# Down projection of a hybrid block: 30 instead of 26 groups by seven products, with two and four weight sums in turn

## The chip, the core and the metric

The kernel runs on one core of a Trainium2 chip. The metric is the device time of one execution in microseconds (us), lower is better. Three runs of the kernel before took 1469.24 to 1470.96 us, with a median of 1470.67 us.

## The reference, cut to what matters

A transformer block with three kinds of attention and a gated feed-forward part works on 256 rows of width 2048, in float32. The change concerns the feed-forward part alone:

```python
h2 = rms_norm(x, g_ffn[l])
u = causal_depthwise_conv(h2 @ w_up[l], conv_w[l], conv_b[l])   # w_up: 2048 x 11264
u_gate, u_val = jnp.split(u, 2, axis=-1)
x = x + (jax.nn.silu(u_gate) * u_val) @ w_down[l]               # w_down: 5632 x 2048
```

## The kernel before, in words

**Numbers in two parts.** TensorE multiplies in a reduced form of float32. So every weight tile is split on the chip: ScalarE casts it (`hi`), VectorE subtracts (`lo`), and one product of two 128-row blocks is three matmuls of 128x512: hi by hi, lo by hi, hi by lo (`three`). A weight tile of 128x1024 is 512 KB.

**The up stage** (lines 1242 to 1267 of the kernel before) runs over 11 blocks of 4 columns of 128, each once for the gate half and once for the value half, and each of these over 8 pieces of `w_up`: 176 pieces in all. A piece is loaded by SyncE's queue into one of 4 buffers (`raw_u`, line 177), cast by ScalarE (`hi_u`, line 180), subtracted by VectorE (`lo_u`, line 181), and used by 8 matmuls of 512 columns (line 1254) and 8 of 256 (line 1256). There are 4 buffers of `hi` and 4 of `lo`, so the piece that is prepared can be up to four ahead of the one that is multiplied. The convolution (`conv`, lines 1135 to 1180) reads the finished banks with ScalarE and VectorE. The order of these instructions on each engine is made by a scheduler, except where the code keeps an instruction in program order.

**The down stage** multiplies 22 groups of two row blocks of `w_down`, in two halves (`nb`) of 1024 output columns. A group can be done in two ways:

- `eight`: 8 products, 24 matmuls, two tiles of 512 KB loaded, cast and subtracted.
- `seven`: a scheme after Strassen with 7 products, 21 matmuls. It needs four sums of the activations ("forms", `FS1` to `FS4`) and four sums of the weights (`T1` to `T4`). It casts and subtracts three and a half tiles.

**The forms** are made in the up stage by VectorE (`forms_of`, `keep_forms`), written to HBM by GpSimd's queue (`kept`), and fetched back in the down stage into ten slots in SBUF (`sf`, 384 KB each, `fetch`). A group that is done by seven products in both halves needs three stored forms; one that is so done in the second half alone needs the fourth as well.

**The weight sums** come in two kinds, by a letter in `PLANS`:

- `t` ("two"): `weight_sums` makes T4 and T2 in the up stage, with 3 additions of 128x512 on VectorE, and GpSimd's queue writes them to HBM as one tile (`T0`, 512 KB). T1 and T3 are added in the down stage by VectorE (line 1371). The group loads 3 tiles of 512 KB.
- `f` ("four"): all four are made in the up stage, with 4 additions, and written as two tiles (`T0` and `T1`). The group loads 256 KB and 3 tiles of 512 KB, and adds nothing in the down stage.

`weight_sums` is a generator that the up stage steps once a piece: one load of 256 KB of `w_down` in each of four steps (buffers `r0`, one copy, and `r1`, two copies), additions in the sixth and seventh, writes in the seventh and eighth. SyncE's queue carries the loads of `r0` and `r1` between those of `raw_u`, and a load into a buffer that is still being written to HBM holds up everything behind it on that queue.

**`PLANS`** gives the order of the groups: `e` is a group by eight, `t` and `f` are groups by seven. Each group becomes two (`e`) or four (`t`, `f`) steps; the loads and casts of a step are issued two steps ahead, and `at(n, ...)` issues a fetch behind step n. Loads from the eleventh on alternate between two pools of four buffers each; the first ten use one pool of four.

Of the kernel before, what the change touches and what calls it, by code (L numbers as in the profile page):

```python
# [34 lines left out]
SBUFS = 4  # L35
BLOCKS = 14
WINDOW = 2
PLANS = ("eeeee" + "tfte" * 3 + "tft" + "ee", "e" + "tte" * 4 + "tfte" + "tftee")
AHEAD = 2
GATE_PLANS = (("e" * 8, "essessee", "essessee"), ("eeesssee", "essessee", "essessee"))  # L40
GATE_SEVENS = 4
# [6 lines left out]
OUT_SEVENS = 3  # L48
KINDS = tuple(plan.replace("e", "") for plan in PLANS)
NSEVEN = tuple(len(kinds) for kinds in KINDS)  # L50
# [8 lines left out]
def hybrid_block(  # L59
# [62 lines left out]
    def later(gen):  # L122
        waiting.append(gen)
# [48 lines left out]
    def piece(src, a, n, name):  # L172
        raw = wp.tile([P, PIECE], F32, tag="raw", name=f"raw_{name}")
        hi = wp.tile([P, PIECE], F32R, tag="hi", bufs=SBUFS, name=f"hi_{name}")
        lo = wp.tile([P, PIECE], F32R, tag="lo", bufs=SBUFS, name=f"lo_{name}")
        m = a * n
        load = nc.sync.dma_start(raw[:, :m].rearrange("p (a n) -> p a n", a=a), src)
        if pinned[0] or in_order[0]:
            tc.keep_in_program_order(load)
        pin(nc.scalar.copy(hi[:, :m], raw[:, :m]))  # L180
        pin(nc.vector.tensor_tensor(lo[:, :m], raw[:, :m], hi[:, :m].bitcast(F32), ALU.subtract))  # L181
        return (
            hi[:, :m].rearrange("p (a n) -> p a n", a=a),
            lo[:, :m].rearrange("p (a n) -> p a n", a=a),
        )
# [924 lines left out]
    def two_banks(name):  # L1110
        return pp2[0].tile([P, 2, 512], F32, tag="pair", name=name)
# [87 lines left out]
    ended = []  # L1199
    made = {}  # L1200
    asked = [(nb, s) for nb in range(2) for s in range(NSEVEN[nb])]
    n_asked = len(asked)

    def weight_sums(nb, s):
        p = ORDERS[nb][s]
        n0 = nb * PIECE
        r = [
            cps[2].tile([P, 2, 512], F32, tag=f"r{j}", bufs=1 + j, name=f"r{j}_{nb}_{p}") for j in range(2)
        ]
        for j, n in ((1, 1), (1, 0), (0, 1), (0, 0)):  # L1210
            tc.keep_in_program_order(
                nc.sync.dma_start(r[j][:, n], dv[:, 2 * p + j, n0 + n * 512 : n0 + (n + 1) * 512])
            )
            yield 1
        yield 1
        add = lambda o, i: tc.keep_in_program_order(nc.vector.tensor_tensor(o, o, i, ALU.add))
        four = KINDS[nb][s] == "f"
        add(r[0][:, 0], r[0][:, 1])
        if four:
            add(r[0][:, 1], r[1][:, 1])  # L1220
        yield 1
        add(r[1][:, 1], r[0][:, 0])
        add(r[1][:, 0], r[1][:, 1])
        made[nb, p] = [dram.tile([P, PIECE], F32, name=f"T{j}_{nb}_{p}") for j in range(1 + four)]
        if four:
            nc.gpsimd.dma_start(made[nb, p][1], r[0].rearrange("p b n -> p (b n)"))
        yield 1
        nc.gpsimd.dma_start(made[nb, p][0], r[1].rearrange("p b n -> p (b n)"))

    adding, n_ticks = [], [0]  # L1230
# [11 lines left out]
    for f0 in range(0, FT, 4):  # L1242
        for s in range(2):
            pairs = [two_banks(f"u{f0 + i}_{s}") for i in (0, 2)]
            c0 = s * D_FF + f0 * P
            for k in range(0, KT, 2):
                hi, lo = piece(upv[:, k : k + 2, c0 : c0 + 512], 2, 512, f"u{f0}_{s}_{k}")
                for j in range(2):
                    first, last = k + j == 0, k + j == KT - 1
                    for i, part in ((0, hi), (1, hi), (0, lo), (1, lo), (2, hi), (3, hi), (2, lo), (3, lo)):  # L1250
                        ps = pairs[i // 2][:, i % 2]
                        c = slice(i * P, (i + 1) * P)
                        if part is hi:
                            nc.tensor.matmul(ps, lhsT=hi[:, j, c], rhs=hT[:, k + j, :], start=first, stop=False)  # L1254
                        else:
                            nc.tensor.matmul(ps[:, :S], lhsT=lo[:, j, c], rhs=hT[:, k + j, :S], start=False, stop=last)  # L1256
                n_ticks[0] += 1
                due = (n_ticks[0] - 8) * n_asked // 164
                if asked and due > n_asked - len(asked):
                    adding.append([weight_sums(*asked.pop(0)), 0])  # L1260
                add_on()
                tick()
            if not cps:
                conv_pool()
            for i in (0, 2):
                later(conv(pairs[i // 2], f0 + i, s))
# [43 lines left out]
    def fetch(p):  # L1310
        slot_of[p] = free_slots.pop(0)
        keep(nc.sync.dma_start(sf[:, slot_of[p]].bitcast(F32), kept[p][:, :, : 3 * P].bitcast(F32).rearrange("p l (f q) -> p l f q", f=3)))
        if p >= NSEVEN[0]:
            keep(nc.sync.dma_start(form_of(p, FS4).bitcast(F32), kept[p][:, :, 3 * P :].bitcast(F32)))
# [152 lines left out]
    def at(n, do):  # L1467
        after_step.setdefault(n, []).append(do)

    to_fetch = list(range(SLOTS, NSEVEN[0])) + list(ORDERS[1][SLOTS:])  # L1470
    for nb, plan in enumerate(PLANS):
        n0 = nb * PIECE
        ns, s = NSEVEN[nb], 0
        X, Y = (lambda nb=nb: banks[nb][0]), (lambda nb=nb: banks[nb][1])
        straight = list(range(FT // 2 - 1, ns - 1, -1)) if nb else list(range(ns, FT // 2))
        n_done = 0
        if nb == 0:
            at(-1, lambda: start(0))
            for p in range(SLOTS):
                at(1 + 2 * p if p < 4 else 3 * p - 4, lambda p=p: fetch(p))  # L1480
        for i, c in enumerate(plan):
            if c != "e":
                p = ORDERS[nb][s]
                seven(p, c, n0, X, Y, s == 0, s == ns - 1)
                if to_fetch and (nb or p < NSEVEN[0] - SLOTS):
                    at(len(steps) + 7, lambda p=p, q=to_fetch.pop(0): (free_slots.append(slot_of.pop(p)), fetch(q)))
                s += 1
                if s == ns:
                    at(len(steps) - 1, lambda nb=nb: later(gather(nb, banks[nb][1])))
            else:  # L1490
                eight(straight.pop(0), n0, X, i == 0, i == len(plan) - 1)
                n_done += 1
                if n_done == 4:
                    at(len(steps) - 1, lambda nb=nb: residual(nb))
        assert s == ns and not straight
        at(len(steps) - 1, finish)
        at(len(steps) - 1, lambda nb=nb: results(nb))
        if nb == 0:
            at(len(steps) - 1, lambda: start(1))
# [45 lines left out]
```

## Time and profile before

| what | value |
|---|---|
| median of three runs | 1470.67 us |
| the profiled execution | 1470.68 us |
| its span (first to last instruction) | 1468.7 us |
| up stage, first to last matmul | 749.6 to 1242.0 us |
| down stage, first to last matmul | 1242.1 to 1464.3 us |
| matmuls of the down stage | 978 |
| granted TensorE clock | 1.00 |

The profile names a group of instructions by line, engine, operation, and tiles as output<-input. `PE` is TensorE, `DVE` VectorE, `ACT` ScalarE, `POOL` GpSimd, `SPq` the queue of SyncE, which issues most of the loads. Matmuls overlap in the records: the time that one costs is read from the starts of successive ones, not from its length. The same holds for VectorE, where the starts of successive instructions lie closer than their lengths.

### The profile page before, as it was taken

How to read it: one execution, taken by the hardware profiler on the slowest of the kernel's cores; microseconds unless marked ns; L12 is line 12 of the kernel's file. 1: busy time of each engine (PE TensorE's matmuls, PEld its weight loads, DVE VectorE, ACT ScalarE, POOL GpSimd, SP SyncE). 2: the span in 40 equal slices, each digit the busy share in tenths (PEclk: the TensorE clock that was granted, in tenths of full speed). 3: DMA queues.
4: the chain of work that ended last, by engine and by line, in shares of the span. 5: the costliest groups of instructions: out<-in, count | busy, mean ns of one | idle time of the engine just before them, and what ended most of it. 6: DMA issues, size and time to landing. Idle time of an engine off the chain costs nothing.

```text
span 1468.7 us, 20884 instructions
## 1 busy us (share of the span) xinstructions
PE 1460.2 (99%) x7315; PEld 1230.6 (84%) x7315; DVE 1210.1 (82%) x1609; ACT 897.6 (61%) x1281; POOL 82.7 (6%) x165
## 2 busy tenths in 40 slices
PE   9999999999999999999999999999999999999998
PEld 7888887888878888888888888888888888888887
DVE  5798766765998799888877888988888888889988
ACT  6755454454664465555667676777676676665664
POOL 1000000021000000000000110100000001000000
PEclk9999999999999999999999999999999999999999
DMA  8698897797666577866766989999988888998985
GB/s 295 200 337 266 264 315 260 225 305 271 233 228 200 204 266 258 284 212 232 276 225 222 305 300 318 300 313 316 297 300 285 289 272 287 397 340 310 339 301 180
DMA packets 172329, 404.82 MB, mean 276 GB/s; under 512 B 14944, under 2 KB 27536, under 8 KB 172224
## 3 DMA queue, kind: packets, MB, share of 16 engines
q1 hardware_dynamic: 156080, 356.62, 72.0%
q0 software_dynamic: 15392, 45.82, 8.5%
q8 instruction: 57, 0.93, 0.3%
q10 hardware_dynamic: 752, 1.06, 0.2%
q14 instruction: 48, 0.39, 0.1%
HBM read 360.97 MB, written 42.47 MB: 275 GB/s over the span
## 4 chain that ended last, share of the span: by engine, by line
PE 96%; DVE 2%; DMA 1%; issue 0%; ACT 0%; SPq 0%; DVEq 0%; ACTq 0%
PE u L1254 22%; PE u L1256 11%; PE d L1325 5%; PE d L1326 5%; PE d L1327 5%; PE g_x L774 4%; PE g_x L775 4%; PE g_x L776 4%; PE f L193 2%; PE f L191 2%; PE f L192 2%; PE s L191 2%; PE s L192 2%; PE s L193 2%; PE b L193 2%; PE b L192 2%
## 5 line engine op out<-in xcount | busy, mean ns | idle before, releaser
L1254 PE MATMUL u<-hT,hi_u 128*128 128x512 f32 x1408 | 442.6, 396 | 0.0
L1256 PEld LDWEIGHTS u<-hT,lo_u 128*128 128x128 f32 x1408 | 264.5, 188 | 62.4
L1256 PE MATMUL u<-hT,lo_u 128*128 128x256 f32 x1408 | 276.9, 278 | 0.0
L181 DVE TENSOR_TENSOR lo_u<-raw_u,hi_u 128x1024 fp32r<-128x1024 f32 x176 | 213.1, 1220 | 47.1 <-ACT hi_u L180 46.3
L180 ACT CAST hi_u<-raw_u 128x1024 fp32r<-128x1024 f32 x176 | 183.4, 1049 | 106.4 <-DMA raw_u<-in_w_up_dram 47.7
L1254 PEld LDWEIGHTS u<-hT,hi_u 128*128 128x128 f32 x1408 | 214.5, 189 | 0.1
L769 ACT CAST hi_g<-raw_g 128x1024 fp32r<-128x1024 f32 (+1 forms) x96 | 91.2, 964 | 55.0 <-PE g_x L775 35.0
L770 DVE TENSOR_TENSOR lo_g<-raw_g,hi_g 128x1024 fp32r<-128x1024 f32 (+1 forms) x96 | 105.0, 1116 | 20.5 <-ACT hi_g L769 20.3
L774 PE MATMUL g_x<-hi_g,xT 128*128 128x512 f32 x251 | 98.8, 394 | 0.0
L775 PE MATMUL g_x<-hi_g,xT 128*128 128x512 f32 x251 | 97.7, 389 | 0.0
L776 PE MATMUL g_x<-lo_g,xT 128*128 128x512 f32 x251 | 96.3, 390 | 0.0
L1153 DVE TENSOR_TENSOR y<-y,z 128x512 f32<-128x512 f32 x88 | 60.7, 690 | 21.5 <-ACT z L1152 18.3
L1152 ACT ACTIVATE z<-u,taps 128x256 f32<-128x256 f32 x176 | 74.7, 496 | 0.0
L180 ACT CAST hi_f<-raw_f 128x1024 fp32r<-128x1024 f32 (+1 forms) x40 | 38.6, 967 | 46.4 <-PE f L192 41.6
L191 PE MATMUL s<-hi_s,xT 128*128 128x512 f32 (+1 forms) x160 | 62.0, 387 | 0.0
L180 ACT CAST hi_s<-raw_s 128x1024 fp32r<-128x1024 f32 (+1 forms) x40 | 38.2, 958 | 36.5 <-PE s L192 30.1
L191 PE MATMUL f<-hi_f,xT 128*128 128x512 f32 (+1 forms) x160 | 60.4, 377 | 0.0
L180 ACT CAST hi_b<-raw_b 128x1024 fp32r<-128x1024 f32 x32 | 33.4, 1052 | 44.2 <-PE b L192 20.1
L193 PE MATMUL s<-lo_s,xT 128*128 128x512 f32 (+1 forms) x160 | 59.1, 370 | 0.0
L193 PE MATMUL f<-lo_f,xT 128*128 128x512 f32 (+1 forms) x160 | 59.0, 369 | 0.0
L192 PE MATMUL f<-hi_f,xT 128*128 128x512 f32 (+1 forms) x160 | 59.0, 369 | 0.0
L192 PE MATMUL s<-hi_s,xT 128*128 128x512 f32 (+1 forms) x160 | 58.9, 368 | 0.0
(494 smaller groups left out, 3306.5 us busy)
## 6 DMA issues: line engine op xcount, KB each, us to landing
raw_u<-in_w_up_dram SPq DMA_DIRECT2D x176, 512.0 KB, 5.9
raw_g<-in_w_in_dram SPq DMA_DIRECT2D x86, 512.0 KB, 5.2
T<-r POOLq DMA_DIRECT2D x62, 512.0 KB, 5.9
r<-in_w_down_dram SPq DMA_DIRECT2D x104, 256.0 KB, 5.5
raw_s<-in_w_down_dram SPq DMA_DIRECT2D x46, 512.0 KB, 6.2
raw_d<-in_w_down_dram SPq DMA_DIRECT2D x36, 512.0 KB, 6.4
raw_f<-in_w_in_dram SPq DMA_DIRECT2D x32, 512.0 KB, 5.2
raw_s<-in_w_in_dram SPq DMA_DIRECT2D x32, 512.0 KB, 5.4
```

Source lines behind the costliest of these rows:

```text
L180: pin(nc.scalar.copy(hi[:, :m], raw[:, :m]))
L181: pin(nc.vector.tensor_tensor(lo[:, :m], raw[:, :m], hi[:, :m].bitcast(F32), ALU.subtract))
L191: nc.tensor.matmul(o, lhsT=xh, rhs=wh, start=first, stop=False)
L192: nc.tensor.matmul(o, lhsT=xl, rhs=wh, start=False, stop=False)
L193: nc.tensor.matmul(o, lhsT=xh, rhs=wl, start=False, stop=last)
L769: pin(nc.scalar.copy(hi[:, :n], src))
L770: pin(nc.vector.tensor_tensor(lo[:, :n], src, hi[:, :n].bitcast(F32), ALU.subtract))
L774: nc.tensor.matmul(o, lhsT=a[0], rhs=w[0], start=first, stop=False)
L775: nc.tensor.matmul(o, lhsT=a[1], rhs=w[0], start=False, stop=False)
L776: nc.tensor.matmul(o, lhsT=a[0], rhs=w[1], start=False, stop=last)
L1254: nc.tensor.matmul(ps, lhsT=hi[:, j, c], rhs=hT[:, k + j, :], start=first, stop=False)
L1256: nc.tensor.matmul(ps[:, :S], lhsT=lo[:, j, c], rhs=hT[:, k + j, :S], start=False, stop=last)
```

## The change

In the first half 14 groups instead of 12 are done by seven products, in the second half 16 instead of 14. Of the 30, 14 are of kind `f` (before: 6 of 26) and 16 of kind `t` (before: 20). The first half begins with four groups by eight instead of five. A weight sum is now begun 5 pieces behind a `t` and 6 behind an `f`, the first at the ninth piece; before, the 26 were spread evenly, 6.3 pieces apart. The first ten fetches of forms stand behind steps 2, 4, ... 20; before, behind 1, 3, 5, 7, 8, 11, 14, 17, 20 and 23.

```diff
-PLANS = ("eeeee" + "tfte" * 3 + "tft" + "ee", "e" + "tte" * 4 + "tfte" + "tftee")
+PLANS = ("eeee" + "tftfte" * 2 + "tftf" + "ee", "e" + "tftfe" * 4 + "e")
...
-    n_asked = len(asked)
+    next_sum = [9]
...
-                due = (n_ticks[0] - 8) * n_asked // 164
-                if asked and due > n_asked - len(asked):
-                    adding.append([weight_sums(*asked.pop(0)), 0])
+                if asked and n_ticks[0] == next_sum[0]:
+                    nb, i = asked.pop(0)
+                    adding.append([weight_sums(nb, i), 0])
+                    next_sum[0] += 6 if KINDS[nb][i] == "f" else 5
...
-                at(1 + 2 * p if p < 4 else 3 * p - 4, lambda p=p: fetch(p))
+                at(2 + 2 * p, lambda p=p: fetch(p))
```

**Place 1: SyncE's queue at the first groups by seven of the down stage.** In these rows `raw_s` are tiles of `w_down` of a group by seven, `raw_t42` and `raw_t13` its sums from HBM, `raw_d` tiles of a group by eight, `sf` a fetch of forms; the numbers behind a name are the half, the group or row block, and a number of the build. Before:

```order
L1307 DMA raw_t42_0_0_12205<-T0_0_0_7469 128x1024
L1312 DMA sf_11952<-kept5_8361 128x768
L1307 DMA raw_s0_2_12225<-in_w_down_dram 128x512
L1307 DMA raw_s0_3_12237<-in_w_down_dram 128x1024
L1307 DMA raw_t13_0_1_12249<-T1_0_1_7648 128x1024
L1307 DMA raw_t42_0_1_12251<-T0_0_1_7647 128x1024
L1312 DMA sf_11952<-kept6_8830 128x768
L1307 DMA raw_s0_4_12271<-in_w_down_dram 128x1024
L1307 DMA raw_s0_5_12283<-in_w_down_dram 128x1024
L1312 DMA sf_11952<-kept7_8835 128x768
L1307 DMA raw_t42_0_2_12298<-T0_0_2_7794 128x1024
L1307 DMA raw_d0_34_12317<-in_w_down_dram 128x1024
```

The same place now:

```order
L1308 DMA raw_t42_0_0_12251<-T0_0_0_7286 128x1024
L1313 DMA sf_12036<-kept3_7909 128x768
L1308 DMA raw_s0_2_12271<-in_w_down_dram 128x512
L1313 DMA sf_12036<-kept4_8380 128x768
L1308 DMA raw_s0_3_12284<-in_w_down_dram 128x1024
L1308 DMA raw_t13_0_1_12296<-T1_0_1_7460 128x1024
L1308 DMA raw_t42_0_1_12298<-T0_0_1_7459 128x1024
L1313 DMA sf_12036<-kept5_8385 128x768
L1308 DMA raw_s0_4_12318<-in_w_down_dram 128x1024
L1313 DMA sf_12036<-kept6_8856 128x768
L1308 DMA raw_s0_5_12331<-in_w_down_dram 128x1024
L1308 DMA raw_t42_0_2_12345<-T0_0_2_7641 128x1024
```

In the eleven rows between the first and the third `raw_t42` four fetches stand instead of three, and behind the third group comes another group by seven, where a group by eight (`raw_d0_34`) came. From the start of the down stage to the load of `raw_d0_36` twelve fetches are issued in both kernels.

**Place 2: VectorE in the third block of the up stage.** `lo_u8_0_8` and `lo_u8_0_10` are two successive pieces; `y` and `aT` belong to the convolution and the forms, `r0` and `r1` to the weight sums. Before:

```order
L181 TENSOR_TENSOR lo_u8_0_8_7921<-raw_u8_0_8_7919,hi_u8_0_8_7920 128x1024
L1186 SCALAR_TENSOR_TENSOR y_4_1_7799<-y_4_1_7799,y_4_0_7571 128x128
L181 TENSOR_TENSOR lo_u8_0_10_7944<-raw_u8_0_10_7942,hi_u8_0_10_7943 128x1024
L1153 TENSOR_TENSOR y_6_1_7816<-y_6_1_7816,z1_6_1_7819 128x512
L1187 TENSOR_TENSOR y_4_0_7571<-y_4_1_7799,y_4_0_7571 128x128
L1153 TENSOR_TENSOR y_6_1_7816<-y_6_1_7816,z0_6_1_7823 128x512
L181 TENSOR_TENSOR lo_u8_0_12_7966<-raw_u8_0_12_7964,hi_u8_0_12_7965 128x1024
```

Now:

```order
L181 TENSOR_TENSOR lo_u8_0_8_7940<-raw_u8_0_8_7938,hi_u8_0_8_7939 128x1024
L1186 SCALAR_TENSOR_TENSOR y_4_1_7819<-y_4_1_7819,y_4_0_7589 128x128
L1216 TENSOR_TENSOR r1_0_4_7764<-r1_0_4_7764,r0_0_4_7763 128x512
L1153 TENSOR_TENSOR y_6_1_7836<-y_6_1_7836,z1_6_1_7839 128x512
L1187 TENSOR_TENSOR y_4_0_7589<-y_4_1_7819,y_4_0_7589 128x128
L1153 TENSOR_TENSOR y_6_1_7836<-y_6_1_7836,z0_6_1_7843 128x512
L1216 TENSOR_TENSOR r1_0_4_7764<-r1_0_4_7764 128x512
L1161 TENSOR_TENSOR y_6_0_7605<-y_6_0_7605,y_6_1_7836 128x512
L1171 TENSOR_TENSOR aT_6836<-y_4_0_7589,aT_6836 128x2x256
L1184 TENSOR_TENSOR y_6_1_7836<-y_6_0_7605 128x256
L181 TENSOR_TENSOR lo_u8_0_10_7966<-raw_u8_0_10_7964,hi_u8_0_10_7965 128x1024
```

Nine instructions instead of one stand between the two pieces. This run of nine occurs once in the kernel before, in the second block. In the changed kernel it occurs four times, in the third, fourth, fifth and eighth blocks, in the last of these with an addition into `r0` first.

## The prediction

> **What bounds the kernel now.** I read the page's busy times and its chain first, then the busy times by stretch, then the starts of TensorE's matmuls, and last who waited for whom in the two stages that change. On the page:
>
> ```profile
> PE 1460.2 (99%) x7315; PEld 1230.6 (84%) x7315; DVE 1210.1 (82%) x1609; ACT 897.6 (61%) x1281; POOL 82.7 (6%) x165
> PE 96%; DVE 2%; DMA 1%; issue 0%; ACT 0%; SPq 0%; DVEq 0%; ACTq 0%
> ```
>
> TensorE is busy for 99% of the span, and 96% of the chain that ended last is its work. A busy TensorE need not be at its pace, so the starts count. In the timeline of the last products:
>
> ```profile
> 1461.19 0.39 PE L1327 MATMUL d<-lo_d,aT 128*128 128x512 f32 x1
> ...
> 1463.91 0.39 PE L1327 MATMUL d<-lo_d,aT 128*128 128x512 f32 x1
> L1325 PE MATMUL d<-hi_d,aT x144: 389/389/470, 1242.1 to 1463.5; 128*128 128x512 f32 x144
> ```
>
> Twelve matmuls lie between these two starts (every third is from line 1327): 2.72 us, 0.227 each. The last row is one line of the stage, with its first and last start. The down stage has 978 matmuls: from the first to the last start 977 x 0.227 = 221.8 us at this pace, and 1463.9 - 1242.1 = 221.8 in the trace. So nothing waits there that costs anything. In the up stage:
>
> ```profile
> L1254 PE MATMUL u<-hT,hi_u x1408: 389/396/478, 749.6 to 1241.6; 128*128 128x512 f32 x176
> ```
>
> 176 pieces of eight such matmuls take 492.0 us, 2.80 a piece, and 1408 of 512 and 1408 of 256 columns at 0.227 and half of that would make 2.72 a piece, so nothing there waits for long either. TensorE sets the time in both stages; all else is cover. How thick the cover is decides the change. By stretch (length, busy time of PE, PEld, DVE, ACT, POOL with counts, clock, share of the DMA engines, GB/s):
>
> ```profile
> 780.00:1130.00 350.00, 350.00 (x2012) 305.42 (x2011) 299.40 (x398) 250.19 (x389) 27.16 (x51) 1.00 0.90 298
> 1242.00:1248.00 6.00, 6.00 (x30) 4.98 (x29) 4.42 (x7) 5.44 (x11) 1.48 (x3) 1.00 0.72 208
> 1248.00:1293.00 45.00, 45.00 (x200) 37.30 (x199) 36.20 (x39) 27.23 (x33) 0.00 (x0) 1.00 1.02 396
> 1293.00:1350.00 57.00, 57.00 (x254) 47.19 (x253) 50.79 (x53) 37.82 (x41) 0.00 (x0) 1.00 0.91 319
> ```
>
> In the up stage VectorE is at 86% and the DMA engines at 0.90; at the start of the down stage the DMA engines are full for 45 us, at 396 GB/s. Those are the two thin places.
>
> **The change part by part.**
>
> *Fewer matmuls.* Four groups go from 24 matmuls to 21: 12 x 0.227 = 2.72 us less, all on the path. This is the whole gain: the span has no other stall that the change could remove, so 1470.68 - 2.72 = 1467.96 is the floor.
>
> *Loads at the head of the down stage.* The views of casts by ScalarE and matmuls at the fourth block by eight before its second run of groups by seven, and of the DMA issues with their size and median time to landing:
>
> ```profile
> 1300.49 2.00 ACT L1320 CAST hi_d<-raw_d 128x1024 fp32r<-128x1024 f32 x2
> 1302.38 0.39 PE L1325 MATMUL d<-hi_d,aT 128*128 128x512 f32 x1
> raw_t<-T SPq DMA_DIRECT2D x32, 512.0 KB, 6.6
> sf<-kept SPq DMA_DIRECT2D x16, 384.0 KB, 8.1
> 1242.27 0.33 SPq L1312 DMA_DIRECT2D sf<-kept  x1
> ```
>
> This is `raw_d0_36`: the first of the two casts is done at about 1301.5, 0.9 us ahead of its matmul. So after 45 us of full DMA the cover had shrunk to 0.9. SyncE's queue could not begin before 1242.27, when the up stage's last matmul freed the slots of the forms. From there to `raw_d0_36` the queue carries, before: 9 tiles of groups by eight (512 KB each), 4 groups `t` (1536 KB) and 2 `f` (1792 KB), and 12 fetches (384 KB): 18,944 KB. Now, with `raw_d0_32` loaded ahead of the first fetch: 4 tiles, 3 `t`, 2 `f` and again 12 fetches: 14,848 KB. That is 4.19 MB less, 10.6 us at 396 GB/s. But TensorE arrives there earlier by two groups by eight and one by seven, 69 x 0.227 = 15.7 us. The loads are 5.1 us short, less the 0.9 of cover: a stall of 4.2 us if the DMA engines do as they did. If the 6 us at 208 GB/s and part of the stretch at 319 are filled, which was room for (396 - 208) x 6 = 1.1 MB or 2.8 us in the first alone, the stall goes to nothing. The bounds are 0 and 4.2; I take 2.7, since the four buffers of the first ten loads hold the queue back as they did, and only half of the slow stretch may be won.
>
> The Trainium skill, on the page DMA: Bandwidth & Descriptors, section "Where 436 GB/s comes from", puts the limit of transfers from HBM at about 358 GB/s a core. By that the same 45 us would carry 4.8 us less and the sum would end near 1476. The trace does not agree: 396 over 45 us. The sum goes by the trace.
>
> *More sums in the up stage.* 16 loads of 256 KB, 12 writes of 512 KB and two forms of 384 KB come in: 11.3 MB over 492 us, 23 GB/s beside 298, so by proportion the DMA share goes from 0.90 to 0.97. VectorE gets 20 additions and two groups' forms:
>
> ```profile
> L1216 DVE TENSOR_TENSOR r<-r 128x512 f32<-128x512 f32 x52 | 35.6, 685 | 2.0 <-DMA r<-in_w_down_dram 1.6
> L1216 DVE TENSOR_TENSOR r<-r,r 128x512 f32<-128x512 f32 x32 | 21.9, 684 | 0.1
> ```
>
> 20 x 0.685 = 13.7 us on VectorE, which has 50 of 350 us free. GpSimd's queue gets the 12 writes and is idle for most of the stage. None of this is on the path as long as each `lo_u` is done before its matmul. Where this was closest before:
>
> ```profile
> 803.26 1.22 DVE L181 TENSOR_TENSOR lo_u<-raw_u,hi_u 128x1024 fp32r<-128x1024 f32 x1
> ...
> 808.74 1.22 DVE L181 TENSOR_TENSOR lo_u<-raw_u,hi_u 128x1024 fp32r<-128x1024 f32 x1
> L181 DVE TENSOR_TENSOR lo_u<-raw_u,hi_u x22: 1215/1220/1227, 744.4 to 808.7; 128x1024 fp32r<-128x1024 f32 x22
> L1256 PE MATMUL u<-hT,lo_u x168: 274/277/364, 750.1 to 810.0; 128*128 128x256 f32 x168
> 810.61 0.40 PE L1256 MATMUL u<-hT,lo_u 128*128 128x256 f32 x2
> ```
>
> The 22nd `lo_u` ends at 809.96; 168 matmuls of line 1256 are 21 pieces, so the 22nd piece's first begins at 810.61. The cover is 0.65 us. It came from the run of nine instructions between two pieces (place 2 of the change): 5.5 us from start to start instead of 2.80. This run stood once; now it stands four times. Entered with full buffers it again leaves about 0.65 and costs nothing. Whether they are full depends on SyncE's queue:
>
> ```profile
> SPq L177 <- DVE lo_u L181: 226.3, 127, 4.6
> SPq L1212 <- DMA T<-r: 70.5, 22, 7.2
> 820.55 0.53 POOL L1226 DMA_DIRECT2D T<-r  x1 [5.54 <-DVE r L1216]
> 819.68 0.37 SPq L177 DMA_DIRECT2D raw_u<-in_w_up_dram  x1
> 827.35 0.90 SPq L1212 DMA_DIRECT2D r<-in_w_down_dram  x2
> ACT hi_u L180 <- DMA raw_u<-in_w_up_dram: 47.7, 35, 4.0
> ```
>
> 22 loads of `r` waited for a write of sums, 3.2 us on average; the longest began after an `f`, whose `T1` still left the single `r0`. What is queued behind such a wait is `raw_u`; who waits for that is ScalarE's cast (47.7 us in 35 times), then VectorE, then TensorE, which so far never did. Sums now stand 5 or 6 pieces apart, not 6.3, and 14 of them are `f`: more such waits, each up to 1.3 x 2.80 = 3.6 us longer. But a wait of SyncE delays only the next load by what exceeds the pace, and the four buffers behind it hold 11.2 us. Bounds: 0 to 4 x 1.0 = 4 us, if each of the four runs is entered 1.6 us poorer (half of 3.2). I take 0.8, near the row where TensorE never waited.
>
> *The down stage's engines.* VectorE's additions of line 1371 fall from 40 to 32, while casts and subtractions rise by half a tile for each of four groups and more:
>
> ```profile
> L1321 DVE TENSOR_TENSOR lo_t<-raw_t,hi_t 128x1024 fp32r<-128x1024 f32 x32 | 39.0, 1221 | 1.9 <-ACT hi_t L1320 0.8
> L1371 DVE TENSOR_TENSOR raw_s<-raw_s 128x512 f32<-128x512 f32 x20 | 13.7, 684 | 0.0
> ```
>
> A changed group needs 1.5 more tiles subtracted: 4 x 1.5 x 1.22 = 7.3 us more, and 8 x 0.685 = 5.5 us less: 1.8 us more in 222, hidden. What was late next there, two groups `t` in a row, is now parted by `f`. I put it at 0.
>
> **The sum** against the profiled execution (1470.68, of which the span is 1468.7, and which lies 0.01 from the median): 1470.68 - 2.72 + 2.7 + 0.8 = 1471.5 us.
>
> **The rivals.**
>
> *The loads keep up.* For it: the queue starts with a tile more in hand, and it was partly idle in the first 6 us. Against it: 0.9 us of cover after 45 full us. Then 1470.68 - 2.72 + 0 to 0.8 = 1468.0 to 1468.8.
>
> *Slower: the up stage loses its cover.* The four runs of nine are entered with `raw_u` late, because the `r` loads in front of them wait for writes on engines at 0.97. It decides from the point where more than 0.65 us of cover is lost ahead of a run. A wait that is longer by the full 3.6 us costs 3.6 - 0.65 = 2.95 in one run; in two of the four, the other two having won their cover back, 5.9. With the loss in the down stage that gives 1470.68 - 2.72 + 2.7 + 5.9 = 1476.6, without it 1473.9, and with all four runs hit 1482. For it: share and distance both go the wrong way. Against it: VectorE's free 14%.
>
> That the change does less than it says is excluded: the program of the changed kernel has 966 matmuls in the down stage, 12 fewer.
>
> **How the numbers follow.** A measurement of this kernel can tell about 0.2% (2.9 us) from no change. The forecast has 0.52; its own range is 1469.0 to 1473.6, from the bounds of its two unknown terms (1470.68 - 2.72 + 1.0 to 5.6). The loads keep up: 0.23; the floor is 2.72 below, so faster by 2.9 needs the noise of the runs as well, 0.05 in all. The slower rival: 0.21. The last 0.04 is for stalls in the down stage over 4.2 us. Slower by over 0.2%: 0.21 + 0.04, and 0.02 from the forecast's upper end, 0.27. The same: the rest, 0.68. The range is 1468.0 (the floor) to 1477.0 (the slower rival with two runs hit); left out are its dearer half and the noise below the floor, under 0.2 together.
>
> **What would show it.** Right: a gap between successive matmuls of the down stage of 1 to 4 us at the third to fifth group by seven of the first half (about 35 to 45 us into the stage), released by ScalarE's cast of a tile that a DMA had just landed, with the DMA share at 1.0 there; and gaps in the up stage of under 1 us in total, in the runs of nine. Wrong: no gap in the down stage (then the loads kept up), or the up stage's 492 us longer by more than 2 (then the slower rival), or a share of the DMA engines in the up stage that stays near 0.90. Any change before 749 us is not from this edit.

## The result and the profile after

The changed kernel takes 1501.86 us (median of four runs, 1501.25 to 1505.12) against 1470.49 us for the kernel before in the same session: a ratio of 1.0218, with a 95% interval of 1.0205 to 1.023. It is 31 us slower. The prediction had 1471.5 us, with 1468.0 to 1477.0 as its range; the result lies far outside it, on the side of the slower rival and past that rival's dearest case.

On the page of the changed kernel, the busy times and the chain that ended last (span 1500.3 us; the profiled execution took 1502.01):

```profile
PE 1469.5 (98%) x7303; PEld 1228.1 (82%) x7303; DVE 1226.0 (82%) x1637; ACT 904.9 (60%) x1291; POOL 91.4 (6%) x181
PE 63%; issue 24%; DMA 6%; DVE 3%; POOL 2%; ACT 1%; SPq 0%; POOLq 0%; DVEq 0%; ACTq 0%
```

TensorE is still "busy" for 98%, but the chain is only 63% its work, where it was 96%. (Its 24% of issue is time for which the profile shows no waiting; what stands behind that isn't to be had from the chain.) The first row by itself would have hidden the loss; the second shows that the end is no longer set by TensorE alone. The starts of the matmuls tell where. One row of the up stage and two of the down stage (count, then min, median and max duration, first and last start):

```profile
L1254 PE MATMUL u<-hT,hi_u x1408: 387/396/629, 748.5 to 1266.8; 128*128 128x512 f32 x176
L1326 PE MATMUL d<-hi_d,aT x112: 389/389/467, 1267.3 to 1494.2; 128*128 128x512 f32 x112
L1328 PE MATMUL d<-lo_d,aT x112: 388/389/397, 1267.8 to 1494.7; 128*128 128x512 f32 x112
```

The up stage takes 518.3 us from first to last start, where it took 492.0: 26.3 us more, though not one matmul of it was changed. The down stage takes 1494.7 - 1267.3 = 227.4 us, where it took 221.8: 5.6 more with 12 matmuls (2.7 us) fewer. Summed over the times between successive starts, less 0.227 each, its stalls are 8.1 us (those over 0.03 us each are counted, here and below). The up stage begins 1.1 us earlier than before, so nothing was lost ahead of it. So there are two losses, the larger in the stage in which the prediction saw almost none.

The same stretches as before by busy time (length, PE, PEld, DVE, ACT, POOL, clock, DMA share, GB/s; the two of the down stage begin 25 us later than before):

```profile
780.00:1130.00 350.00, 337.74 (x1910) 290.98 (x1909) 290.68 (x393) 233.69 (x365) 32.06 (x60) 0.99 0.89 301
1267.00:1273.00 6.00, 6.00 (x29) 4.96 (x28) 5.38 (x7) 5.11 (x10) 0.00 (x0) 1.00 0.79 250
1273.00:1318.00 45.00, 42.79 (x180) 32.82 (x179) 35.20 (x39) 28.01 (x35) 0.00 (x0) 1.00 0.98 373
```

In the 350 us of the up stage TensorE issued 1910 matmuls instead of 2012. VectorE did less, not more, in that time, and the DMA engines moved 301 GB/s at a share of 0.89, where they had moved 298 at 0.90. More was asked of them, and the stage grew longer at the same rate. That rate alone doesn't say whether they could not do more or were not asked in time. SyncE's queue is the next thing to read, first its two largest waits and then what ScalarE and TensorE waited for (in the groups of the page: busy, mean ns, idle before, and what released most of it):

```profile
SPq L177 <- DVE lo_u L181: 186.0, 103, 6.1
SPq L1212 <- DMA T<-r: 129.6, 35, 8.2
```

```profile
L180 ACT CAST hi_u<-raw_u 128x1024 fp32r<-128x1024 f32 x176 | 183.9, 1049 | 134.7 <-DMA raw_u<-in_w_up_dram 108.2
L1256 PEld LDWEIGHTS u<-hT,lo_u 128*128 128x128 f32 x1408 | 263.9, 189 | 87.3 <-DVE lo_u L181 26.4
L1256 PE MATMUL u<-hT,lo_u 128*128 128x256 f32 x1408 | 280.3, 280 | 17.7 <-DVE lo_u L181 17.5
```

SyncE's waits for a free raw buffer (line 177) are its good waits: they mean that the buffers are full. They fell from 226.3 to 186.0 us. Its waits at the load of `r` for a write of sums rose from 70.5 us in 22 cases to 129.6 in 35. Behind these, ScalarE's cast waited 108.2 us for `raw_u` where it had waited 47.7, and TensorE's weight load waited 26.4 us for `lo_u` where it had never waited; the matmuls behind these loads stood 17.5 us for it. So the stage's loss goes with late `lo_u`. For an `r` that had not landed VectorE itself waited only 0.5 us in the whole stage.

**One stall, followed back.** The longest is at 859 us, in the third block, at the run of nine of place 2. The rows come from the timelines of five engines (start, duration; in brackets the idle time before and its releaser). GpSimd issues `T1` of the fourth sum, an `f`; then SyncE's queue; then ScalarE's casts; then VectorE; then TensorE:

```profile
834.27 0.53 POOL L1226 DMA_DIRECT2D T<-r  x1 [10.65 <-DVE r L1216]
```

```profile
836.34 0.37 SPq L177 DMA_DIRECT2D raw_u<-in_w_up_dram  x1
841.51 0.83 SPq L1212 DMA_DIRECT2D r<-in_w_down_dram  x2
842.44 0.46 SPq L177 DMA_DIRECT2D raw_u<-in_w_up_dram  x1
843.94 0.81 SPq L1212 DMA_DIRECT2D r<-in_w_down_dram  x2
844.84 1.05 SPq L177 DMA_DIRECT2D raw_u<-in_w_up_dram  x2
```

```profile
851.73 1.05 ACT L180 CAST hi_u<-raw_u 128x1024 fp32r<-128x1024 f32 x1 [2.01 <-DMA raw_u<-in_w_up_dram]
852.68 1.09 ACT L1148 ACTIVATE y<-u,taps 128x256 f32<-128x256 f32 x2
853.68 1.70 ACT L1152 ACTIVATE z<-u,taps 128x256 f32<-128x256 f32 x4
```

```profile
850.95 1.22 DVE L181 TENSOR_TENSOR lo_u<-raw_u,hi_u 128x1024 fp32r<-128x1024 f32 x1
...
854.61 0.69 DVE L1153 TENSOR_TENSOR y<-y,z 128x512 f32<-128x512 f32 x1 [1.64 <-ACT z L1152]
...
858.16 1.22 DVE L181 TENSOR_TENSOR lo_u<-raw_u,hi_u 128x1024 fp32r<-128x1024 f32 x1
```

```profile
859.44 0.80 PE L1256 MATMUL u<-hT,lo_u 128*128 128x256 f32 x2 [4.15 <-DVE lo_u L181]
```

The write issued at 834.27 lets go of the only `r0` 7.2 us later, at 841.5. SyncE stood there for 4.8 us, and behind the pair of `r` stood two more loads of `r` and the `raw_u` of the next pieces. The `raw_u` issued at 844.84 landed at 851.7. The convolution's `z` stands behind this late cast in ScalarE's order, and VectorE stood 1.64 us at an addition that needs it. The run of nine grew from 5.5 us (start to start) to 7.2, and TensorE waited 4.15. Even at 5.5 us such a run takes 2.7 longer than a piece of 2.80, so it needs that much in hand; here nothing was, for TensorE had already stood 0.45 us for the `lo_u` ahead of it. The other runs of nine took 6.75, 8.00 and 6.28 us; the four stalls are 4.3, 0.7, 2.5 and 2.1 us (time between starts less 0.25): 9.5 us.

The longest stall had a second price. Two matmuls of 512 columns on TensorE, shortly before it and shortly after:

```profile
853.96 0.63 PE L1254 MATMUL u<-hT,hi_u 128*128 128x512 f32 x2
861.31 1.05 PE L1254 MATMUL u<-hT,hi_u 128*128 128x512 f32 x2
```

The granted clock was 0.50 from 857.5 to 864.3, and such matmuls started 0.43 us apart instead of 0.23. TensorE worked 4.8 us at that clock, which by this estimate cost another 2.4. It is the only such drop in the up stage of this kernel; behind the other three runs of nine the clock stayed at 1.00. The rest of the loss, about 14 us, lies in shorter runs, mostly of four to eight instructions.

### The profile page after: what moved, and what is told of

Same layout as the page of the kernel before. It is cut to its first block, busy times and chain, and to the rows that moved or that the text cites. A ratio compares the mean times of both kernels' runs of the same rounds, so it can differ in the third digit from the quotient of the medians.

```text
span 1500.3 us, 21040 instructions
## 1 busy us (share of the span) xinstructions
PE 1469.5 (98%) x7303; PEld 1228.1 (82%) x7303; DVE 1226.0 (82%) x1637; ACT 904.9 (60%) x1291; POOL 91.4 (6%) x181
## 4 chain that ended last, share of the span: by engine, by line
PE 63%; issue 24%; DMA 6%; DVE 3%; POOL 2%; ACT 1%; SPq 0%; POOLq 0%; DVEq 0%; ACTq 0%
PE g_x L774 4%; PE g_x L775 4%; PE g_x L776 4%; PE u L1254 4%; PE d L1326 4%; PE d L1328 3%; PE d L1327 3%; PE s L191 2%; PE s L193 2%; PE f L193 2%; PE f L192 2%; PE f L191 2%; PE s L192 2%; DMA raw_s<-in_w_down_dram 2%; PE u L1256 2%
## 5 line engine op out<-in xcount | busy, mean ns | idle before, releaser
L1256 PEld LDWEIGHTS u<-hT,lo_u 128*128 128x128 f32 x1408 | 263.9, 189 | 87.3 <-DVE lo_u L181 26.4
L1256 PE MATMUL u<-hT,lo_u 128*128 128x256 f32 x1408 | 280.3, 280 | 17.7 <-DVE lo_u L181 17.5
L180 ACT CAST hi_u<-raw_u 128x1024 fp32r<-128x1024 f32 x176 | 183.9, 1049 | 134.7 <-DMA raw_u<-in_w_up_dram 108.2
L1322 DVE TENSOR_TENSOR lo_s<-raw_s,hi_s 128x512 fp32r<-128x512 f32 (+1 forms) x60 | 56.3, 954 | 12.8 <-ACT hi_s L1321 11.1
L1321 ACT CAST hi_s<-raw_s 128x512 fp32r<-128x512 f32 (+1 forms) x60 | 49.2, 833 | 24.6 <-DMA raw_s<-in_w_down_dram 13.4
L191 PE MATMUL s<-hi_s,xT 128*128 128x512 f32 (+1 forms) x160 | 61.9, 387 | 0.0
L191 PE MATMUL f<-hi_f,xT 128*128 128x512 f32 (+1 forms) x160 | 60.4, 377 | 0.0
```

Of the source, the lines that this page charges most:

```text
L191: nc.tensor.matmul(o, lhsT=xh, rhs=wh, start=first, stop=False)
```

## The experiments

The theory that stood after the traces, called *loop* below: an addition frees `r` only through a write of 6 to 7 us; the next load of `r` waits for that write in SyncE's queue, in order; `raw_u` behind it comes late; the later `raw_u` delays the next addition. When the sums come closer, the turn no longer fits into the time between two sums. The rivals: VectorE cannot take the additions; the kind `f` with its second write is to blame; the DMA engines cannot carry the bytes; and SyncE as the place of the wait matters by itself. Lengths of the up stage are from first to last start of its 512-column matmuls, stalls of the down stage are the times between successive starts less 0.227, summed.

**1. The loads of `r` on GpSimd's queue.**

```
-                nc.sync.dma_start(r[j][:, n], ...)
+                nc.gpsimd.dma_start(r[j][:, n], ...)
```

> The changed kernel with the loads of r0 and r1 issued by GpSimd's queue instead of SyncE's, all else as it is. Up stage now: 518.7 us (before 492.4), down stage 227.4. Queue theory (raw_u is late because it stands behind loads of r that wait for writes of sums, 129.6 us of waiting in 35 times): SyncE has no such waits left, the stalls of TensorE in the up stage go, 492 to 500 us, total 1474 to 1483. VectorE theory (the 20 additions and their places fill VectorE): the order on VectorE hardly moves, so 512 to 520, total 1495 to 1503. Traffic theory (11 MB more on the DMA engines): nothing is saved, 515 to 520, total about 1500.

Measured: 1545.77 us, 1.051 times before (1.0479 to 1.054); the up stage took 563.2 us. SyncE no longer waited for writes at all, and yet it was worse. In the waits of this kernel up to 1240 us:

```profile
DVE r L1216 <- DMA r<-in_w_down_dram: 57.8, 23, 8.3
POOL r L1212 <- DMA T<-r: 27.7, 14, 3.9
```

On GpSimd the loads stand behind the issue of writes that wait for additions, so now `r` comes late, and VectorE stands at the addition (57.8 us in 23 cases) with the `lo_u` behind it. The edit moves the wait instead of removing it, and the theory can't be judged by it; none of the three expected ranges held. What it shows: with the wait on GpSimd's queue the additions come late, and with them the `lo_u` behind them.

**2. The additions on 16 of 512 columns** (the sums are not made).

```
-        add = lambda o, i: ...tensor_tensor(o, o, i, ALU.add))
+        add = lambda o, i: ...tensor_tensor(o[:, :16], o[:, :16], i[:, :16], ALU.add))
```

> The changed kernel with the additions of the weight sums in the up stage done on 16 of 512 columns, so that the sums are not made; every load, write and wait stays. VectorE loses about 104 x 0.55 = 57 us of work in the up stage, more than the change added. VectorE theory: the stalls go, up stage 492 to 497 us, total 1474 to 1480. Queue theory: the writes can start a little sooner (1 to 2 us a sum), so a part goes, up stage 505 to 515, total 1487 to 1497. Traffic theory: 515 to 520, total about 1500.

Measured: 1500.85 us, 1.0204 (1.0146 to 1.0262); up stage 523.0 us. An addition fell from 0.685 to 0.171 us:

```profile
L1216 DVE TENSOR_TENSOR r<-r 128x16 f32<-128x16 f32 x60 | 10.2, 171 | 3.2 <-DMA r<-in_w_down_dram 2.6
SPq L1212 <- DMA T<-r: 142.4, 40, 9.7
```

104 additions x 0.514 = 53 us less work on VectorE changed nothing: 523.0 us lies above all three expected ranges. SyncE's waits for writes stayed. The amount of VectorE's work is not the cause.

**3. and 4. The number of `f`.** Third kernel: 30 groups, but only six of them `f`; its sums stand a little closer, 5.2 pieces apart. Fourth: the plan of before with its 26 groups and its spacing, but ten `f` instead of six. (The expectation says 14 and eight more; the plan has ten, and the trace 36 writes of sums in the up stage, 26 and ten.)

```
+PLANS = ("eeee" + "tftfte" * 2 + "tttt" + "ee", "e" + "tftte" * 2 + "tttte" * 2 + "e")
```

```
+PLANS = ("eeeee" + "tfte" * 3 + "tft" + "ee", "e" + "tfe" * 4 + "tfte" + "tftee")
```

> The changed kernel, 30 groups, but 6 of kind f and 24 of kind t, as few f as before: 8 writes of T1 and 8 additions fewer, r0 held for a write 6 times instead of 14, and a sum begun every 5.2 pieces. Queue theory: the waits on r0 fall by about half, those on r1 stay or grow, up stage 503 to 513 us. VectorE theory: 12 instead of 20 additions more than before, up stage 505 to 512. Traffic theory: 7 instead of 11 MB more, 505 to 510. If the f kind is what hurts, under 500. The down stage may lose 1 to 3 us by two t in a row. Total 1485 to 1500.

> The kernel before, 26 groups evenly 6.3 pieces apart, with 14 groups of kind f instead of 6: 8 more writes of T1, 8 more additions, r0 held 14 times; number of groups, spacing and fetches stay. Queue theory: the distance of 6.3 keeps the waits on r1 as they were, eight more on r0 of 3 to 7 us each; up stage 493 to 500 us, total 1471 to 1479. VectorE theory: 8 more additions of 0.6 us, up stage 492 to 500. Traffic theory: 4 MB more, 492 to 502. If the f kind is what hurts: over 505.

Measured: 1503.6 us, 1.0223 (1.0193 to 1.0253), up stage 519.9 us, for the third; 1472.0 us, 1.001 (0.9998 to 1.0022), up stage 495.1, for the fourth, with SyncE waiting 88.8 us for writes. With six `f` the loss is whole, above every range expected for it; four more `f` at the old spacing cost 3 us of the stage. So the kind `f` is not what the loss needs. What 14 `f` would cost at the old spacing was not run.

**5. Writes of sums that don't hold `r`** (from `hT`, behind a 16-column copy on GpSimd; the sums are made and not written).

```
-            nc.gpsimd.dma_start(made[nb, p][1], r[0]...)
+            nc.gpsimd.tensor_copy(mark, r[0][:, 1, :16])
+            nc.gpsimd.dma_start(made[nb, p][1], hT[:, 2:4]...)
```

> The changed kernel with the same writes of sums at the same places, but from the activations hT instead of from r (a copy of 16 columns on GpSimd waits for the additions in the write's place), so that r0 and r1 are not held for a write; the sums in HBM are not the right ones. DMA traffic, additions and order stay. Loop theory (additions, write, next load of r, next raw_u, cast, subtraction: about 18 us a turn, over 5 to 6 pieces, slower than TensorE's 2.80 a piece): the write leaves the loop, up stage 492 to 498 us, total 1474 to 1480. Traffic theory: up stage 512 to 520, total 1495 to 1502.

Measured: 1525.93 us, 1.0379 (1.0334 to 1.0423); up stage 537.9. The expectation of *loop* (492 to 498) was missed, and that of the traffic theory (512 to 520) as well. But the edit brought a wait of its own: the copies stand in GpSimd's order behind the writes of the forms, which wait for ScalarE.

```profile
POOL kept L1196 <- ACT y L1193: 163.5, 15, 25.5
SPq L1212 <- POOL mark L1231: 32.4, 16, 6.1
```

GpSimd waited up to 25.5 us for a form, and SyncE waited for the copies behind it. So this run decides nothing, as the first did; it took a buffer's release from a DMA and gave it to a queue that was late.

**6. Closeness alone: the kernel before, its 26 sums every 5.5 pieces instead of every 6.3.**

```
-                due = (n_ticks[0] - 8) * n_asked // 164
+                due = (n_ticks[0] - 8) * 30 // 164
```

> The kernel before with its 26 sums begun every 5.5 instead of every 6.3 pieces, so that they end some 20 pieces earlier; loads, writes, additions and groups are those of before. Loop theory: 2.95 instead of 2.80 us a piece while sums are made (some 140 pieces), up stage 508 to 516, total 1487 to 1496. A theory by which the total of work or of traffic in the stage is too much: 492 to 496, total 1470 to 1475.

Measured: 1493.23 us, 1.0156 (1.012 to 1.0192), by one number changed in the kernel before. Its up stage, and SyncE's waits for writes in it:

```profile
L1254 PE MATMUL u<-hT,hi_u x1408: 389/396/628, 748.9 to 1262.3; 128*128 128x512 f32 x176
SPq L1212 <- DMA T<-r: 111.0, 28, 7.7
```

513.4 us: 21.4 of the 26.3 us, with the additions, writes and matmuls of before. The number of the sums is not the cause; their distance is. (While it lasts, this kernel asks for bytes as densely as the changed one, so that bytes per time stay a rival.)

**7. and 8. More distance, and later fetches.** In the seventh kernel the four loads of `r` go out in two steps instead of four, the first of them two pieces later, so that those of `r1` stand further behind the write that they wait for (of the two of `r0`, one comes a piece later too). In the eighth, for the down stage, the first ten fetches come every four steps instead of every two, and four later ones eight steps later.

```
-        for j, n in ((1, 1), (1, 0), (0, 1), (0, 0)):
+        yield 1
+        yield 1
+        for j, n in ((1, 1), (1, 0), (0, 1), (0, 0)):
...
-            yield 1
+            if n == 0:
+                yield 1
```

```
-                at(2 + 2 * p, lambda p=p: fetch(p))
+                at(2 + 4 * p, lambda p=p: fetch(p))
...
-                    at(len(steps) + 7, ...
+                    at(len(steps) + (7 if nb else 15), ...
```

> The changed kernel with the four loads of a sum issued in two steps instead of four, the loads of r1 so one to two pieces later behind the write that frees their buffer; those of r0, additions and writes stay where they are. Loop theory: the loop's 18 us now span 7 pieces, 2.6 us each, below TensorE's pace: up stage 493 to 502 us, total 1475 to 1484. Traffic or VectorE theory: 515 to 520, total about 1500.

> The changed kernel with the first ten fetches of forms every four steps instead of every two, and the following four of the first half eight steps later: 8 instead of 12 fetches ahead of the load of raw_d0_36, 1.6 MB less in the full stretch. Shortage of loads at the head of the down stage (4.2 us of gaps in five groups by seven there): those gaps go to under 1 us, down stage 223 to 224.5 instead of 227.4; the 3.5 us of gaps in the second half stay. If the fetches have no part in it: 227. Up stage unchanged at 517 to 521, total 1497 to 1499.

Measured: 1491.89 us, 1.0147 (1.0118 to 1.0176), for the seventh: the up stage 510.8 us, SyncE's waits for writes 87.0. Better by 7.5 us in the stage, but far from the 493 to 502 of *loop*, and why it is not better still was not found. The sum of SyncE's waits alone doesn't give the loss: with 87.0 us of them this stage loses 18.8 us, that of the fourth kernel with 88.8 loses 3.1. For the eighth 1501.03 us, 1.0209 (1.018 to 1.0239): the down stage's stalls fell from 8.1 to 6.0 us. At 30 to 50 us into the stage they fell from 4.2 to 1.9, but 2.0 came up at 60 to 77, so that the first half gained almost nothing. The drop came from 130 us on (3.6 to 1.4), where none was expected.

**9. A second `r0` and a third `r1`.** The last four columns of `aT` are written only at the end of the up stage; until then their 8 KB a partition serve as one more buffer of each kind. Bytes, additions and plan are those of the changed kernel.

```
+        q = nb * NSEVEN[0] + s
         r = [
+            ff.tile([P, 2, 512], F32, tag=f"spare{j}", ...) if q < 25 and q % (2 + j) == 1 + j else
             cps[2].tile([P, 2, 512], F32, tag=f"r{j}", bufs=1 + j, ...) for j in range(2)
         ]
```

> The changed kernel, with one more r0 buffer and one more r1 buffer (4 KB a partition each) in the place of the last four columns of aT, which are written only at the end of the up stage; 25 of the 30 sums take turns between these and the old buffers. The same bytes, the same additions, the same plan; only a load of r no longer stands behind a write of sums that has just begun. Theory loop (SyncE's queue waits for writes of sums, and raw_u behind it comes late): SyncE's waits of 129.6 us for writes of sums fall under 30, the up stage goes from 518.7 back to 492 to 498, and the total to 1474 to 1481 us, the down stage staying at 226 to 228. Theory traffic (the DMA engines or VectorE cannot carry 30 sums at a spacing of 5 or 6 pieces): the up stage stays at 512 to 520, the total at 1494 to 1503.

Measured: 1476.82 us, 1.0053 (1.0035 to 1.007). The up stage, SyncE's waits for writes, and the stretch of 350 us:

```profile
L1265 PE MATMUL u<-hT,hi_u x1408: 389/396/500, 750.0 to 1245.7; 128*128 128x512 f32 x176
SPq L1223 <- DMA T<-r: 22.1, 7, 6.6
780.00:1130.00 350.00, 349.33 (x2004) 304.14 (x2003) 309.29 (x422) 250.15 (x391) 33.06 (x62) 1.00 0.93 318
```

495.7 us: 22.6 of the 26.3 us are gone. The clock drop is gone too. The DMA engines now move 318 GB/s at a share of 0.93, and VectorE works 309 of 350 us, both more than in any kernel above. So neither was at its end in the changed kernel: they were asked too late. The runs of nine take 5.49 us again, and the first three of the four cost nothing; the last costs 0.5. *Loop* had it right here, and *the DMA engines cannot carry it* falls. (The down stage took 224.2 us, below the expected 226 to 228.)

**10. Fewer bytes with the waits kept:** loads of `r`, after the first into each buffer, of 16 of 512 columns.

```
-                nc.sync.dma_start(r[j][:, n], ...)
+                nc.sync.dma_start(r[j][:, n, : 512 if q <= j else 16], ...)
```

> The changed kernel, with every load of r after the first of each buffer cut to 16 of its 512 columns, so that the sums added are not those of the weights (a part of the computation is left out); additions and writes of sums stay whole. About 30 MB of some 156 MB of the up stage are not moved, but every load of r still stands behind the write that frees its buffer. Theory loop: SyncE's waits for writes of sums stay over 90 us and the up stage at 505 to 519, the total at 1487 to 1502. Theory traffic: with a fifth less to move the up stage falls to 490 to 498, the total to 1472 to 1481.

Measured: 1473.76 us, 1.0028 (1.0015 to 1.004). The up stage, SyncE's waits, the stretch, and three rows of its DMA issues (KB each, median us to landing):

```profile
L1256 PE MATMUL u<-hT,hi_u x1408: 389/396/478, 748.1 to 1240.1; 128*128 128x512 f32 x176
SPq L1214 <- DMA T<-r: 95.9, 34, 6.6
780.00:1130.00 350.00, 350.00 (x2011) 305.39 (x2011) 311.96 (x424) 250.69 (x392) 34.66 (x65) 1.00 0.81 255
raw_u<-in_w_up_dram SPq DMA_DIRECT2D x170, 512.0 KB, 4.8
T<-r POOLq DMA_DIRECT2D x44, 512.0 KB, 5.3
r<-in_w_down_dram SPq DMA_DIRECT2D x114, 8.0 KB, 3.4
```

Here *loop*, as it was stated, missed, and the range of the traffic theory held: SyncE still waited 95.9 us in 34 cases, and the up stage took 492.0 us, no loss at all. Here the waits cost nothing, and what stood behind them landed sooner: `raw_u` took 4.8 us instead of 6.4, a write of sums 5.3 instead of 6.6, a load of `r` 3.4 instead of 5.2. Every part of the turn got shorter, and the DMA engines, at 0.81, may have had room to make good what was held. The ninth and tenth runs together show that the loss takes the waits *and* the full loads of `r`. Take away either, and the stage is back within 4 us. Why the bytes matter stays open: the two effects of this edit, a shorter turn and more room, are not told apart, and run 9 moved more bytes per time than any kernel with the loss.

**11. and 12. The two halves of the plan apart,** both with the spare buffers: the eleventh with the first half's plan of before and the second half's of the changed kernel, the twelfth the other way round; 28 groups by seven and 972 matmuls in the down stage each.

```
+PLANS = ("eeeee" + "tfte" * 3 + "tft" + "ee", "e" + "tftfe" * 4 + "e")
```

```
+PLANS = ("eeee" + "tftfte" * 2 + "tftf" + "ee", "e" + "tte" * 4 + "tfte" + "tftee")
```

> The kernel with spare buffers for r (now for 28 sums), but with the first half's plan of before (12 groups by seven, 5 by eight at its head) and the second half's plan of the changed kernel: 28 groups by seven, 972 matmuls in the down stage, 220.2 us at 0.227 each. Theory head (the stalls 30 to 50 us into the down stage come of two groups by eight fewer in the first half, with the first ten fetches as before; those at 130 us come of the second half's plan): 0.3 us of stalls in the first half, 1.4 at 130 us, the down stage 221.9; with an up stage of 493 to 496 the total is 1470.5 to 1474. Theory end (the stalls are what the up stage's backlog of loads and writes leaves behind): 2 to 3.5 us of stalls remain 30 to 50 us into the stage, the down stage 224.

> The kernel with spare buffers for r (for 28 sums), with the first half's plan of the changed kernel (14 groups by seven) and the second half's plan of before (14): 28 groups by seven, 972 matmuls in the down stage, 220.2 us. Theory head: 3.5 us of stalls 30 to 50 us into the down stage as in the run with spare buffers, 0.3 at the bank switch, none at 130 us, the down stage 224.0, the total 1472.5 to 1476. Theory end: the same stalls 30 to 50 us into the stage in both kernels of this pair, and at 130 us too.

Measured: 1473.65 us, 1.0029 (1.002 to 1.0038), and 1472.23 us, 1.0017 (1.0008 to 1.0026), the latter 0.3 us below the range of *head*. The 45 us from six us into the down stage, first of the eleventh and then of the twelfth kernel:

```profile
1249.00:1294.00 45.00, 45.00 (x200) 37.29 (x199) 35.87 (x39) 27.74 (x33) 0.00 (x0) 1.00 0.98 364
```

```profile
1249.00:1294.00 45.00, 43.17 (x184) 33.37 (x183) 36.05 (x40) 27.39 (x34) 0.00 (x0) 1.00 0.97 370
```

With the old first half TensorE doesn't wait there (200 matmuls, as before); with the new one it does (184). By the starts: the eleventh has no stall 30 to 50 us into the stage and 1.6 us at 130; the twelfth has 3.6 us at 30 to 50 and none at 130. *Head* is borne out in this pair, and *end* falls. But the old first half alone does not exclude the stall: the fourth kernel has it too, and in its profiled execution TensorE lost 2.0 us at 37 to 41 us into the stage, with 366 GB/s in the 45 us. The up stages take 493.9 and 495.3 us. No kernel of the study beats the one before.

## Why the prediction was wrong

**Fewer matmuls, -2.72 us.** Right as far as it goes: the page has 7303 matmuls instead of 7315, at the same pace where nothing waits. It is a gain that the two other terms swallowed.

**More sums in the up stage, +0.8 us (bounds 0 to 4).** This is the step that failed: 26.3 us. The prediction found the right wait (`r` behind a write in SyncE's queue), saw that it would come more often and last longer, named who stands behind it, and then dropped it with one sentence: "a wait of SyncE delays only the next load by what exceeds the pace, and the four buffers behind it hold 11.2 us". Three things in it were wrong. The four buffers don't hold 11.2 us of landed data: from issue to landing a `raw_u` takes 6.4 us here (median), so that by this estimate 11.2 - 6.4 = 4.8 us of them are landed, and SyncE's wait in the stall shown above was 4.8 us by itself, with a wait for the next `r` behind it. (It is an estimate and no threshold: tiles already cast and subtracted add to it, and a wait of 7.2 us in the kernel before cost nothing.) The delay isn't paid once and then won back: sums come every 5 or 6 pieces, and the cover was not refilled in between (runs 9 and 10 show that more buffers for `r`, or fewer bytes, end it). And the delay does not stay with `raw_u`: the convolution stands behind the late cast in the order of ScalarE and VectorE. The bound of 4 us counted only the four runs of nine, at 1 us each; they cost 9.5, the drop of the clock behind one of them about 2.4, and the rest, over half, fell outside them. The table of work per engine, VectorE at 86%, was read rightly and was beside the point (run 2).

Nor was the row "near" which the value was taken a bound. TensorE never waited in the kernel before, but 70.5 us of waits in SyncE's queue and a closest cover of 0.65 us said that it was near the point where it would. Run 6 shows how near: the same kernel with sums 0.8 pieces closer loses 21 us.

**The share of the DMA engines.** Expected was 0.97 by proportion; it stayed at 0.89, since the stage stretched. The prediction had put "a share that stays near 0.90" down as a sign that it was wrong, and so it was. The reading "by proportion" assumes that the stage keeps its length.

**Loads at the head of the down stage, +2.7 us (bounds 0 to 4.2).** The mechanism was right, at the place that was named. In the changed kernel, at the last product of one group and the first of the next, 39 us into the stage (ScalarE, then TensorE):

```profile
1306.95 1.99 ACT L1321 CAST hi_t<-raw_t 128x1024 fp32r<-128x1024 f32 x2 [2.50 <-DMA raw_t<-T]
```

```profile
1306.58 0.40 PE L1328 MATMUL d<-lo_s,aT 128*128 128x512 f32 x1
1308.05 0.50 PE L1326 MATMUL d<-hi_t,sf 128*128 128x512 f32 x1 [1.07 <-ACT hi_t L1321]
```

A tile that a DMA had just landed, a cast that waited 2.50 us for it, and a matmul behind the cast. The stalls from 30 to 50 us into the stage are 4.2 us in the changed kernel and 3.5 in run 9: the term was mis-sized, near its upper bound, and not at 2.7. The first 6 us were filled better, as hoped (0.79 and 250 GB/s, before 0.72 and 208), but the 45 us after them moved 373 GB/s, not the 396 on which the sum rested. The Trainium skill, on the page DMA: Bandwidth & Descriptors, section "Where 436 GB/s comes from", has about 358 GB/s for transfers from HBM; the 373 of this stretch and the 364 of run 11, where TensorE waited for nothing, lie between that and the 396 of the kernel before.

**The down stage's engines, 0 us.** Wrong by 3.6 us in the changed kernel: 0.5 to 1.8 us are lost 130 us into the stage in every kernel with the new second half, and nothing in the kernels with the old one (before, runs 6 and 12). In the changed kernel another 1.8 us go 150 to 170 us into the stage; run 9 has none there, and why was not looked into.

**The rivals.** The slower rival named the mechanism: runs of nine entered with `raw_u` late because `r` waits for writes. Its price for a run, 2.95 us, was fair (9.5 us in four); its total was too low, because it let the cover come back between the runs, and over half of the loss lies there. Its chance of 0.21 was too small for a mechanism with every sign in the profile. The rival that the loads keep up is refuted by the stalls above. The forecast's own range was also narrower than its terms: it took 1.0 to 5.6 us for the two unknown ones, whose stated bounds add up to 0 to 8.2; the measured stalls are 26.3 and 4.2.

## What to carry to other kernels

A load that must wait for a write-back stands in one queue with all loads behind it: count, per turn, addition, write, load and the loads behind it against the time to the next turn, and ask whether the buffers are full again before the next turn. Here they were not, and 0.8 pieces less distance cost 21 us in a kernel where TensorE had never waited. The sum of the queue's waits says little by itself: 87.0, 88.8 and 95.9 us went with losses of 18.8, 3.1 and 0 us (runs 7, 4 and 10). Two more buffers, found in memory that is not written until later, were worth 25 us (1501.86 to 1476.82); moving the wait to another queue made it worse.

## What the runs showed of the hardware

- The share of the DMA engines was not proportional to bytes: 318 GB/s at 0.93 with sums (run 9), 255 at 0.81 when 114 loads were 8 KB (run 10), 396 at 1.02 and 373 at 0.98 at the head of the down stage. So a share could not be scaled here from one mix of transfers to another.
- The time to landing moved with the load: 512 KB of `raw_u` took 6.0 us before, 6.4 in the changed kernel, and 4.8 in run 10, with a fifth of all bytes gone though its own were the same.
- A DMA issue took GpSimd longer than SyncE: 0.545 us on average for the 120 loads of `r` in run 1, against 0.441 on SyncE in the changed kernel.
- The granted clock fell to 0.50 behind some waits of TensorE, for 3.4 or 6.8 us each time: in the up stage once in the changed kernel, six times in run 1, and not at all in the kernel before and in runs 9 and 10. A wait then costs more than its own length.
